# One more split pair from the start, seven more seven-product pairs, and the residual rows back in two halves

## The chip, the cores and the metric

The kernel runs on one core of a Trainium2 chip. A core has five engines that each work through their own list of instructions in order: PE (matmul), DVE (vector), ACT (scalar and activation), POOL (general) and SP, which here only starts DMAs. They meet through semaphores: an instruction waits until another engine has counted far enough, and everything behind it on its engine waits too. The metric is device time in microseconds of one execution, the median of several.

## The reference

One decoder layer on x of 256 tokens by 2048, in float32:

```python
u = RMSNorm(h);  lru_x, lru_gate, q, k, v, ret_gate = split(u @ w_in)
y = concat(RG-LRU(conv(lru_x)) * gelu(lru_gate),  retention(q, k, v) * silu(ret_gate))
h = h + y @ w_out                                  # 2048 x 2048
u = RMSNorm(h)
h = h + (silu(u @ w_gate) * (u @ w_up)) @ w_down   # 2048 x 5632 twice, 5632 x 2048
out = RMSNorm(h)
```

## The kernel before

**Precision.** Every float32 operand x is split into xh, a cast to a 32-bit matmul type (`fp32r`), and xl = x - xh. A product is three matmuls: ah bh, ah bl, al bh (`three`, L683 to L685). A weight tile thus comes as a DMA of 128 x 1024 into a raw tile (SP), is cast by ACT into `wh` (L123), and subtracted by DVE into `wl` (L124). Raw tiles rotate through 6 buffers, the pairs `wh`/`wl` through 4; from gate/up 1 to gate/up 9 there are 2 more of each (`raw2`, `split2`). A cast can start only when PE has read the last product from the pair that had the buffer before.

**Blocks.** The three late projections work on 2 x 2 blocks of the result (c11, c12, c21, c22, each 128 tokens by 512 columns, a bank of PSUM): out has two blocks (0, 1), gate/up eleven (0 to 10; c11 and c21 are gate, c12 and c22 up), down two (0, 1). A "quad" is one step along the contraction: 256 rows of weights by 1024 columns, two raw loads b11, b12 and b22, b21, against a left of a11, a12, a21, a22. A plain quad is eight products, 24 matmuls. A pair that is "summed" needs seven (Strassen in Winograd's form), 21 matmuls, and for that four sums of lefts (`sh`, `sl`) and four DVE adds of raw weights (`add`, L661), a split more, and a reload of half the weights.

**Sharing.** The products that several summed pairs of a block have in common are accumulated ahead, while the block before is still in work. `STEPS` gives for each block a string of steps: p is a plain quad, h half of one, s the "shared" part of a summed pair of the *next* block (four products, four raw adds, splits of 512, 512, 1024 and 512 columns), d the "direct" part of a pair of this block (three products, one load, one split of 1024). After the last s the results are combined (`share`, L806 to L811): p1 is a copy of c11 by ACT (L806), p = c12 - p1 and q = p - c22 by DVE (L807, L808), then q is copied by ACT back onto c12's PSUM tile (L809), and DVE forms c22 and c21 (L810, L811). PE's plain and direct products are then added onto these tiles; its first product onto c12 must wait for the copy L809. I call the step from one block to the next a handover. `SUMMED` lists the summed pairs: 2 in out 1, 2 in gate/up 0, 3 in gate/up 1, 4 in each of gate/up 2 to 9, 3 in gate/up 10, 3 shared ones (0, 1, 2) ahead of down 0. In down 5 more pairs are summed in block 0 and 7 in block 1, each as a `Quad` with all its seven products in one step (`SUMMED_DOWN`, in the order `ORDER_DOWN`).

**After a block.** In out, `post` adds the result to the residual rows (htok, DVE, L597), squares them (ACT), stores them to memory (`kept_rows`) and transposes them for gate/up (`turn`: PE into `ht`, ACT to `hf`, then cast and split, `ah` and `al`). In gate/up ACT forms silu (`gated`, L874), DVE multiplies (L876), PE transposes, ACT copies (`ff`, L867). Before down all eight row tiles (256 KB each) and the weights of the last norm are loaded back by POOL's queue (`swap_back`); `down_post` adds and normalises.

**Order.** The program is a list of steps. Loads are emitted three ahead of the step in work (`AHEAD`), and a scheduler that goes through the steps with its own timeline fixes the order of instructions on each engine when the kernel is built. On the chip each engine keeps to that order.

## Time and profile before

| | before |
|---|---|
| median of 3 runs | 1082.41 us (1081.9 to 1084.11) |
| profiled execution | 1082.46 us, span 1080.7 us |
| PE busy | 1070.2 us, 99%, 5089 matmuls |
| DVE busy | 964.1 us, 89% |
| ACT busy | 664.5 us, 61% |
| PE waits in all | 2.8 us |
| DMA | 244.62 MB, mean 226 GB/s |

Busy is the share of the span in which an engine had an instruction in work. A matmul counts as busy until its modelled end, though the next starts earlier, so 99% says that PE hardly stood still, not that it ran at its peak. In a timeline a row has the start in us, the duration, engine, line, operation and tiles (out<-in), and in brackets the idle time before it with what ended it. A row of waits has the waiting line, the one waited for, and the us in total, the times and the longest. The clock granted to PE was full throughout.

### The profile page before, as it was taken

To read this page: it belongs to the slowest core of one execution; us is meant where nothing else is said; L and a number is where in the kernel's file an instruction comes from. 1 tells how busy PE (TensorE), PEld (TensorE's weight loads), DVE (VectorE), ACT (ScalarE), POOL (GpSimd) and SP (SyncE) were. 2 spreads that over 40 slices of the span, in tenths; PEclk is the share of its full clock that TensorE was granted. 3 is DMA by queue.
4 is the path that set the end of the run, shared out by engine and by line. 5 is a ranking of instruction groups with operands and counts; after the bars stand their busy time and mean duration, and the time that the engine had idled before them with its cause. 6 is when DMAs were issued, how large, how long until landed. Compare 5 with 4: busy or idle time off the path is not lost.

```text
span 1080.7 us, 14590 instructions
## 1 busy us (share of the span) xinstructions
PE 1070.2 (99%) x5089; PEld 897.7 (83%) x5089; DVE 964.1 (89%) x1399; ACT 664.5 (61%) x947; POOL 57.2 (5%) x73
## 2 busy tenths in 40 slices
PE   9999999999999999999999999999999999999997
PEld 7888888888888888888888888888888888888886
DVE  7889789988878889989999999999999889997886
ACT  7666644468756676656656565665656656654563
POOL 0602230000000000000000000000002000000001
PEclk9999999999999999999999999999999999999999
DMA  9965475554556588677776777777767856474662
GB/s 325 336 213 171 159 254 166 183 176 158 192 195 234 183 304 273 231 235 256 257 270 228 251 260 242 263 269 232 258 234 270 289 181 214 162 245 159 214 212 101
DMA packets 71386, 244.62 MB, mean 226 GB/s; under 512 B 8208, under 2 KB 8592, under 8 KB 71312
## 3 DMA queue, kind: packets, MB, share of 16 engines
q1 hardware_dynamic: 68400, 236.34, 64.6%
q0 software_dynamic: 1472, 4.72, 1.3%
q10 hardware_dynamic: 1440, 2.62, 0.6%
q8 instruction: 40, 0.66, 0.2%
q14 instruction: 34, 0.28, 0.1%
HBM read 239.46 MB, written 4.19 MB: 225 GB/s over the span
## 4 chain that ended last, share of the span: by engine, by line
PE 98%; DVE 1%; DMA 1%; POOL 0%; SPq 0%; ACT 0%; issue 0%; POOLq 0%; ACTq 0%
PE c L685 22%; PE c L683 22%; PE c L684 22%; PE fm L194 11%; PE fm L196 5%; PE tm L174 3%; PE tm L175 3%; PE tm L176 3%; PE p L683 1%; PE p L685 1%; PE p L684 1%; PE ft L865 1%; DMA x<-in_x 1%; PE ht L588 0%; PE sc L492 0%; DVE wl L124 0%
## 5 line engine op out<-in xcount | busy, mean ns | idle before, releaser
L123 ACT CAST wh<-raw 128x1024 fp32r<-128x1024 f32 (+1 forms) x498 | 462.9, 959 | 323.8 <-PE c L685 130.8
L124 DVE TENSOR_TENSOR wl<-raw,wh 128x1024 fp32r<-128x1024 f32 (+1 forms) x498 | 542.2, 1115 | 72.5 <-ACT wh L123 71.2
L684 PE MATMUL c<-wl,ah 128*128 128x512 f32 x826 | 322.7, 391 | 0.0
L685 PE MATMUL c<-wh,al 128*128 128x512 f32 x826 | 321.8, 390 | 0.0
L683 PE MATMUL c<-wh,ah 128*128 128x512 f32 x826 | 280.3, 391 | 0.0
L683 PEld LDWEIGHTS c<-wh,ah 128*128 128x128 f32 x826 | 155.1, 188 | 32.0 <-ACT wh L123 0.3
L685 PEld LDWEIGHTS c<-wh,al 128*128 128x128 f32 x826 | 155.2, 188 | 31.8
L684 PEld LDWEIGHTS c<-wl,ah 128*128 128x128 f32 x826 | 155.2, 188 | 31.6
L194 PE MATMUL fm<-u,wh 128*128 128x512 f32 x512 | 161.4, 396 | 0.0
L196 PEld LDWEIGHTS fm<-u,wl 128*128 128x128 f32 x512 | 96.1, 188 | 22.4
L196 PE MATMUL fm<-u,wl 128*128 128x256 f32 x512 | 101.2, 279 | 0.0
L661 DVE TENSOR_TENSOR raw<-raw,raw 128x512 f32<-128x512 f32 x114 | 78.4, 689 | 2.0
L661 DVE TENSOR_TENSOR raw<-raw 128x512 f32<-128x512 f32 x114 | 78.3, 688 | 1.4
L194 PEld LDWEIGHTS fm<-u,wh 128*128 128x128 f32 x512 | 78.4, 189 | 0.3
L684 PE MATMUL c<-wl,sh 128*128 128x512 f32 x192 | 74.3, 390 | 0.0
L685 PE MATMUL c<-wh,sl 128*128 128x512 f32 x192 | 73.7, 390 | 0.0
L683 PE MATMUL c<-wh,sh 128*128 128x512 f32 x192 | 67.3, 391 | 0.3 <-ACT sh L123 0.3
L176 PE MATMUL tm<-wh,u 128*128 128x512 f32 x128 | 48.7, 391 | 0.0
L175 PE MATMUL tm<-wl,u 128*128 128x512 f32 x128 | 48.7, 393 | 0.0
L174 PE MATMUL tm<-wh,u 128*128 128x512 f32 x128 | 46.9, 394 | 1.4 <-ACT u L298 1.4
L683 PEld LDWEIGHTS c<-wh,sh 128*128 128x128 f32 x192 | 36.1, 188 | 8.1 <-ACT sh L123 0.7
L685 PEld LDWEIGHTS c<-wh,sl 128*128 128x128 f32 x192 | 36.1, 188 | 7.5
(247 smaller groups left out, 1027.4 us busy)
## 6 DMA issues: line engine op xcount, KB each, us to landing
raw<-in_w_gu SPq DMA_DIRECT2D x216, 512.0 KB, 5.3
raw<-in_w_down SPq DMA_DIRECT2D x91, 512.0 KB, 4.6
raw<-in_w_out SPq DMA_DIRECT2D x34, 512.0 KB, 3.7
raw<-in_w_lx SPq DMA_DIRECT2D x16, 512.0 KB, 6.4
raw<-in_w_k SPq DMA_DIRECT2D x16, 512.0 KB, 3.6
raw<-in_w_q SPq DMA_DIRECT2D x16, 512.0 KB, 4.2
raw<-in_w_rg SPq DMA_DIRECT2D x16, 512.0 KB, 3.5
raw<-in_w_lg SPq DMA_DIRECT2D x16, 512.0 KB, 3.5
```

Source lines behind the costliest of these rows:

```text
L123: act.copy(out=dst_h, in_=src)
L124: v.tensor_tensor(out=dst_l, in0=src, in1=dst_h.bitcast(F32), op=ALU.subtract)
L174: pe.matmul(ps, ah, wh, start=first, stop=False)
L175: pe.matmul(ps, ah, wl, start=False, stop=False)
L176: pe.matmul(ps, al, wh, start=False, stop=last)
L194: pe.matmul(ps, wh, hl, start=n + i == 0, stop=False)
L196: pe.matmul(ps[:, :S], wl, hl[:, :S], start=False, stop=n + i == len(order) - 1)
L661: v.tensor_tensor(out=dst, in0=a, in1=b, op=ALU.add)
L683: pe.matmul(p, ah, bh, start=first, stop=False, skip_group_check=onto)
L684: pe.matmul(p, ah, bl, start=False, stop=False, skip_group_check=onto)
L685: pe.matmul(p, al, bh, start=False, stop=last, skip_group_check=onto)
L865: pe.transpose(pt[:, o : o + P], g[:, (2 * b + c) * P : (2 * b + c) * P + P], ident)
```

## The change

- `SUMMED`, `STEPS`: out 1 gets four summed pairs (4 to 7) for two, gate/up 0 three (1, 2, 3) for two, gate/up 1 and gate/up 10 four for three: five more pairs with seven products. The steps of the blocks that host the shared parts change with them.
- Down 1 gets two more summed pairs, 12 and 19, and an order in which summed and plain quads alternate. The sums of these two lefts, made in down 0 for pairs 12 and 19, are kept in a pool of their own (`sums`) until step 7 of down 1.
- Pools: one more split pair, `split_near`, from out 0 to step 5 of down 1; one more split pair and two raw tiles, `split_far` and `raw_far`, from gate/up 1 to step 6 of down 0. Before it was two and two from gate/up 1 until the start of gate/up 10. The rows' pool moves to the other side of the memory, and a pad of 96 bytes stands ahead of it.
- The rows come back in two halves of four tiles: after step 9 of down 0 and after step 7 of down 1; the weights of the last norm after step 8 of down 1.

In the program as built PE has 21 matmuls fewer, all of 512 columns. DVE has 28 more raw adds, 19 more splits of 512 and 2 of 1024 columns, and 8 sums of 128 columns; ACT 19 more casts of 512 and 2 of 1024; SP 5 more loads of 512 KB. Split and raw tiles start at multiples of 128 bytes in both programs. All lines move by 5 to 8: L123 becomes L128, L661 L666, L806 L813, L809 L816.

```diff
--- before.py
+++ after.py
@@ -29,16 +29,17 @@
 
-SUMMED = ((), (4, 5), (2, 3), (1, 2, 3)) + ((0, 1, 2, 3),) * 8 + ((1, 2, 3),)
-SUMMED_OUT, SUMMED_FFN = (4, 5), (0, 1, 2, 3)
+SUMMED = ((), (4, 5, 6, 7), (1, 2, 3)) + ((0, 1, 2, 3),) * 10
+SUMMED_OUT, SUMMED_FFN = (4, 5, 6, 7), (0, 1, 2, 3)
 
 PLAIN = ((4, 5, 6, 7, 0, 1, 2, 3),) * 2 + (tuple(range(8)),) * 11
-STEPS = ("pppspppspp", "ppspdpsdpp", "pdpsdpspspp", "pspsdpsdpsdp") + ("psdhsdhsdhsdhp",) * 7 + ("psdpsdpsddp", "psdpsdpsdpp")
+STEPS = ("ppspspspsppp", "psdpsdpsddp", "pspsdpsdpsdp") + ("psdhsdhsdhsdhp",) * 9 + ("psdpsdpsddp",)
 
 EARLY_DOWN = (0, 1, 2)
-SUMMED_DOWN = (9, 12, 15, 17, 19), (5, 7, 9, 11, 13, 15, 17)
-ORDER_DOWN = (3, 4, 0, 5, 6, 1, 7, 8, 2) + tuple(range(9, 22)), tuple(range(22))
+SUMMED_DOWN = (9, 12, 15, 17, 19), (5, 7, 9, 11, 12, 13, 15, 17, 19)
+ORDER_DOWN = (3, 4, 0, 5, 6, 1, 7, 8, 2) + tuple(range(9, 22)), (0, 12, 1, 19, 2, 5, 3, 7, 4, 9, 6, 11, 8, 13, 10, 15, 14, 17, 16, 18, 20, 21)
+BESIDE = (12, 19)
 
 @with_exitstack
@@ -48,14 +49,17 @@
 
     cpool = ctx.enter_context(tc.tile_pool(name="consts", bufs=1))
     apool = ctx.enter_context(tc.tile_pool(name="acts", bufs=60))
+    edge = ctx.enter_context(tc.tile_pool(name="edge", bufs=1, side="right"))
+    edge.tile([P, 24], F32, name="edge_pad")
+    kept_stack = ctx.enter_context(ExitStack())
+    xpool = kept_stack.enter_context(tc.tile_pool(name="resid", bufs=8, side="right"))
     rpool = ctx.enter_context(tc.tile_pool(name="raw", bufs=6))
     wpool = ctx.enter_context(tc.tile_pool(name="split", bufs=4))
     early = ctx.enter_context(ExitStack())
-    xpool = early.enter_context(tc.tile_pool(name="resid", bufs=8))
     epool = early.enter_context(tc.tile_pool(name="conv", bufs=2))
     tpool = early.enter_context(tc.tile_pool(name="tmp", bufs=6))
-    late, resid, more, turn_of = [], [xpool], [], [0, 0]
-    extra = ExitStack()
+    late, resid = [], [xpool]
+    more_raw, more_split, counts = [], [], [0, 0]
     pmm = ctx.enter_context(tc.tile_pool(name="pmm", bufs=4, space=PSUM))
     paux = ctx.enter_context(tc.tile_pool(name="paux", bufs=4, space=PSUM))
 
@@ -72,14 +76,15 @@
         return resid[0].tile([P, 512], dt, tag="xh", name=nm(name))
 
     def split_tiles():
-        turn_of[1] += 1
-        pool_ = more[1] if more and turn_of[1] % 3 == 0 else wpool
-        return [pool_.tile([P, 1024], F32R, tag=g, name=nm(g)) for g in ("wh", "wl")]
+        counts[0] += 1
+        n = counts[0] % (4 + len(more_split))
+        p = more_split[n - 4] if n >= 4 else wpool
+        return [p.tile([P, 1024], F32R, tag=g, name=nm(g)) for g in ("wh", "wl")]
 
     def raw_tile():
-        turn_of[0] += 1
-        pool_ = more[0] if more and turn_of[0] % 4 == 0 else rpool
-        return pool_.tile([P, 1024], F32, tag="raw", name=nm("raw"))
+        counts[1] += 1
+        p = more_raw[0] if more_raw and counts[1] % 4 == 0 else rpool
+        return p.tile([P, 1024], F32, tag="raw", name=nm("raw"))
 
     def late_tile(name, dt=F32):
         return late[0].tile([P, 512], dt, tag="late", name=nm(name))
@@ -551,7 +556,7 @@
 
         names = ("a11", "a21", "a12", "a22", "s1", "s2", "s3", "s4")
 
-        def __init__(self, f, sums):
+        def __init__(self, f, sums, place=act_tile):
             self.h, self.l = [act_tile("ah", F32R)], [act_tile("al", F32R)]
             split(self.h[0], self.l[0], f)
             if sums:
...
@@ -726,6 +731,8 @@
 
         for i in range(n):
             program.append(([quads[i]], step(i)))
+            if i in hooks[ordered]:
+                program.append(([], hooks[ordered][i]))
 
         def end():
             with tc.manual_schedule(engines={nc.tensor.engine}) if ordered else ExitStack():
@@ -902,7 +909,8 @@
 
     def make_left(p):
         if dl[p] is None:
-            dl[p] = Left(ff[p], p in EARLY_DOWN + SUMMED_DOWN[0] + SUMMED_DOWN[1])
+            place = sum_tile if p in BESIDE else act_tile
+            dl[p] = Left(ff[p], p in EARLY_DOWN + SUMMED_DOWN[0] + SUMMED_DOWN[1], place)
 
     def down_block(d, ahead):
         ps = {} if d else ahead.ps
...
@@ -1094,23 +1102,58 @@
     for n in range(NLRU):
         fm_tile(Unit(A["w_lg"][n]), u, range(KT), lambda ps, n=n: lru_out(n, ps))
 
-    def swap():
+    near, far = ExitStack(), ExitStack()
+
+    def near_begins():
 
         early.close()
-        more.append(extra.enter_context(tc.tile_pool(name="raw2", bufs=2)))
-        more.append(extra.enter_context(tc.tile_pool(name="split2", bufs=2)))
-
-    def stop_more():
-        more.clear()
-
-    def swap_back():
-        extra.close()
-        late.append(ctx.enter_context(tc.tile_pool(name="late", bufs=4)))
-        resid[0] = ctx.enter_context(tc.tile_pool(name="resid2", bufs=8))
-        for key in [(cb, t) for cb in range(4) for t in range(2)]:
+        more_split.append(near.enter_context(tc.tile_pool(name="split_near", bufs=1, reuse_waits="tile")))
+
+    def near_stops():
+        more_split.clear()
+
+    def near_ends():
+        near.close()
+        late.append(ctx.enter_context(tc.tile_pool(name="late", bufs=4, reuse_waits="tile")))
+        load_fw()
+
+    def far_begins():
+
+        kept_stack.close()
+        more_split.append(
+            far.enter_context(tc.tile_pool(name="split_far", bufs=1, side="right", reuse_waits="tile"))
+        )
+        more_raw.append(
+            far.enter_context(tc.tile_pool(name="raw_far", bufs=2, side="right", reuse_waits="tile"))
+        )
+
+    def far_stops():
+        more_split.pop()
+        more_raw.clear()
+
+    beside, sums_kept = ExitStack(), []
+
+    def sum_tile(name, dt):
+        return sums_kept[0].tile([P, 512], dt, tag="sum", name=nm(name))
+
+    def rows_back(d):
+        resid[0] = ctx.enter_context(tc.tile_pool(name=f"resid_{d}", bufs=4, side="right", reuse_waits="tile"))
+        for key in [(cb, t) for cb in (2 * d, 2 * d + 1) for t in range(2)]:
             htok[key] = res_tile("htok")
             pool.dma_start(out=htok[key], in_=kept[key])
-        load_fw()
+
+    def far_ends():
+        far.close()
+        rows_back(0)
+        sums_kept.append(
+            beside.enter_context(tc.tile_pool(name="sums", bufs=4, side="right", reuse_waits="tile"))
+        )
+
+    def sums_end():
+        beside.close()
+        rows_back(1)
+
+    hooks = {0: {6: far_stops, 9: far_ends}, 1: {5: near_stops, 8: near_ends, 7: sums_end}}
 
     blocks = [Block(d, lambda i, d=d: A["w_out"][8 * d + i], y, out_post(d), STEPS[d], SUMMED[d]) for d in range(2)]
     blocks += [
@@ -1119,12 +1162,11 @@
     ]
     down = Block(NB + 2, lambda i: A["w_down"][i], dl, None, "", EARLY_DOWN, make_left)
     for b, after in zip(blocks, blocks[1:] + [down]):
+        if b.index == 0:
+            program.append(([], near_begins))
         if b.index == 3:
-            program.append(([], swap))
-        if b.index == NB + 1:
-            program.append(([], stop_more))
+            program.append(([], far_begins))
         b.put(after)
-    program.append(([], swap_back))
 
     for d in range(2):
         down_block(d, down)
```

Three places at handovers, as the built orders have them. First ACT at the handover from gate/up 9 to 10, from before, where c12_1588 is the tile that q is copied onto and wh_1630 and wh_1633 are the first weights that PE multiplies onto it:

```order
L123 CAST wh_1630_7774<-raw_1629_7772 128x1024
L123 CAST wh_1633_7789<-raw_1632_7787 128x1024
L123 CAST wh_1641_7808<-raw_1635_7793 128x512
L123 CAST ah_1636_7795<-ff_925_4524 128x512
L809 COPY c12_1588_7574<-q_1625_7750 128x512
L123 CAST wh_1646_7850<-raw_1635_7793 128x1024
L123 CAST wh_1651_7860<-raw_1650_7858 128x1024
```

The same place in the changed program, ACT, where the tile is c12_1614 and the first weights are wh_1664:

```order
L128 CAST wh_1664_7882<-raw_1663_7880 128x1024
L128 CAST ah_1670_7906<-ff_954_4622 128x512
L128 CAST wh_1685_7971<-raw_1684_7969 128x1024
L128 CAST wh_1692_8015<-raw_1691_8013 128x1024
L816 COPY c12_1614_7651<-q_1659_7858 128x512
```

and PE there:

```order
L690 MATMUL c22_1531_7270<-wh_1655_7840,al_872_4227 128x512
L688 MATMUL c22_1531_7270<-wh_1661_7867,ah_871_4226 128x512
L689 MATMUL c22_1531_7270<-wl_1662_7868,ah_871_4226 128x512
L690 MATMUL c22_1531_7270<-wh_1661_7867,al_872_4227 128x512
L688 MATMUL c11_1611_7639<-wh_1664_7882,ah_859_4190 128x512
L688 MATMUL c12_1614_7651<-wh_1664_7882,ah_859_4190 128x512
```

Before, two later casts (wh_1646, wh_1651) stood behind the copy; now two that take the buffers of wh_1655 and wh_1661 stand ahead of it, and PE reads these for the last time 5 and 2 matmuls ahead of its first product onto c12_1614.

Second, at the handover from gate/up 10 to down, ACT in the changed program; c12_1700 is down's c12, wh_1754 its first weight tile and ah_1752 its first left:

```order
L128 CAST wh_1767_8328<-raw_1766_8326 128x1024
L128 CAST wh_1757_8282<-raw_1756_8280 128x1024
L128 CAST wh_1754_8267<-raw_1751_8261 128x1024
L128 CAST wh_1770_8334<-raw_1769_8332 128x1024
L128 CAST ah_1752_8263<-ff_1037_5002 128x512
L128 CAST wh_1782_8391<-raw_1776_8376 128x1024
L816 COPY c12_1700_8037<-q_1747_8239 128x512
```

and PE there:

```order
L690 MATMUL c21_1699_8033<-wh_1732_8175,sl_1728_8151 128x512
L690 MATMUL c12_1700_8037<-wh_1729_8154,sl_1728_8151 128x512
L690 MATMUL c22_1612_7643<-wh_1743_8221,al_872_4227 128x512
L688 MATMUL c22_1612_7643<-wh_1749_8248,ah_871_4226 128x512
L689 MATMUL c22_1612_7643<-wl_1750_8249,ah_871_4226 128x512
L690 MATMUL c22_1612_7643<-wh_1749_8248,al_872_4227 128x512
L688 MATMUL c11_1697_8025<-wh_1754_8267,ah_1752_8263 128x512
```

Six casts stand here ahead of the copy, and wh_1757, which takes the buffer of wh_1732, stands ahead of wh_1754, the first tile that PE wants.

Third, DVE at the handover from out 1 to gate/up 0, before; c22_775 and c21_776 are gate/up 0's tiles, the htok rows those that out 1 adds to:

```order
L807 TENSOR_TENSOR p_802_3940<-c12_777_3814,p1_801_3939 128x512
L124 TENSOR_TENSOR wl_806_3951<-raw_804_3948,wh_805_3950 128x1024
L124 TENSOR_TENSOR wl_809_3966<-raw_807_3963,wh_808_3965 128x1024
L808 TENSOR_TENSOR q_803_3941<-p_802_3940,c22_775_3806 128x512
L124 TENSOR_TENSOR wl_812_3972<-raw_810_3969,wh_811_3971 128x1024
L810 TENSOR_TENSOR c22_775_3806<-q_803_3941,c21_776_3810 128x512
L811 TENSOR_TENSOR c21_776_3810<-c21_776_3810,p_802_3940 128x512
L124 TENSOR_TENSOR wl_815_4002<-raw_813_3999,wh_814_4001 128x1024
L597 TENSOR_TENSOR htok_611_3053<-c11_677_3369,htok_611_3053 128x512
L597 TENSOR_TENSOR htok_623_3114<-c21_679_3377,htok_623_3114 128x512
```

and in the changed program, where they are c22_791 and c21_792 and the first weights wl_836 and wl_839:

```order
L129 TENSOR_TENSOR wl_839_4089<-raw_837_4086,wh_838_4088 128x1024
L602 TENSOR_TENSOR htok_617_3075<-c11_677_3360,htok_617_3075 128x512
L602 TENSOR_TENSOR htok_629_3136<-c21_679_3368,htok_629_3136 128x512
L129 TENSOR_TENSOR wl_842_4095<-raw_840_4092,wh_841_4094 128x512
L602 TENSOR_TENSOR htok_640_3194<-c12_680_3372,htok_640_3194 128x512
L602 TENSOR_TENSOR htok_652_3255<-c22_678_3364,htok_652_3255 128x512
L666 TENSOR_TENSOR raw_840_4092<-raw_840_4092 128x512
L814 TENSOR_TENSOR p_829_4048<-c12_793_3873,p1_828_4047 128x512
L129 TENSOR_TENSOR wl_836_4074<-raw_834_4071,wh_835_4073 128x1024
L666 TENSOR_TENSOR raw_840_4092<-raw_840_4092,raw_849_4148 128x512
L815 TENSOR_TENSOR q_830_4049<-p_829_4048,c22_791_3865 128x512
L666 TENSOR_TENSOR raw_849_4148<-raw_840_4092,raw_849_4148 128x512
```

The combinations of gate/up 0 stood ahead of the adds onto htok; now p and q, the split wl_836 and three raw adds stand behind them.

More of the change, by code (lines that the diff above doesn't have):

```diff
@@ L564, in __init__ @@
                 v.tensor_tensor(out=s4, in0=a12, in1=s2, op=ALU.subtract)
-                self.h.append(act_tile("sh", F32R))
-                self.l.append(act_tile("sl", F32R))
+                self.h.append(place("sh", F32R))
+                self.l.append(place("sl", F32R))
                 split(self.h[1], self.l[1], g)
@@ L975, in down_post @@
         src = h if src is None else src
-        f = fw[cb][:, c0 : c0 + cw]
+        f = None if cb < 2 else fw[cb][:, c0 : c0 + cw]
         n = cb + (c0 > 0)
@@ L982, in down_post @@
             if cb < 2:
-                defer(13 + 2 * cb + t, lambda: v.tensor_tensor(out=h, in0=h, in1=f, op=ALU.mult))
+                defer(13 + 2 * cb + t, lambda: v.tensor_tensor(out=h, in0=h, in1=fw[cb], op=ALU.mult))
                 return
```

## The prediction

> **What bounds the kernel now.** I read the page first, then the waits of PE (the matmul engine), then timelines at one handover between blocks.
>
> ```profile
> span 1080.7 us, 14590 instructions
> PE 1070.2 (99%) x5089; PEld 897.7 (83%) x5089; DVE 964.1 (89%) x1399; ACT 664.5 (61%) x947; POOL 57.2 (5%) x73
> PEclk9999999999999999999999999999999999999999
> PE 98%; DVE 1%; DMA 1%; POOL 0%; SPq 0%; ACT 0%; issue 0%; POOLq 0%; ACTq 0%
> ...
> PE tm L174 <- ACT u L298: 1.4, 2, 1.0
> PE warm L116 <- DVE eps_t L109: 1.1, 1, 1.1
> PE c L683 <- ACT sh L123: 0.3, 1, 0.3
> ```
>
> PE is busy 99% of the span, the chain that ended last is 98% PE, and PE's whole list of waits is 2.8 us, 2.5 of them at the start. So the time is the number of matmuls times their spacing, and every wait that the change brings onto PE is paid in full. DVE, at 89%, is close behind.
>
> ```profile
> 600.79 0.39 PE L684 MATMUL c<-wl,ah 128*128 128x512 f32 x1
> 601.02 0.39 PE L685 MATMUL c<-wh,al 128*128 128x512 f32 x1
> ...
> 601.92 0.39 PE L685 MATMUL c<-wh,al 128*128 128x512 f32 x1
> ...
> 603.74 0.62 PE L683 MATMUL c<-wh,ah 128*128 128x512 f32 x2
> ...
> 370.74 0.40 PE L683 MATMUL c<-wh,sh 128*128 128x512 f32 x1
> 371.43 0.50 PE L683 MATMUL c<-wh,sh 128*128 128x512 f32 x1 [0.30 <-ACT sh L123]
> ```
>
> Five spacings from 600.79 to 601.92 are 1.13 us, so one matmul of 512 columns costs 0.227 us, while its result is complete 0.39 us after its start. The last two rows are the one stall in the middle of the run: 0.69 us from start to start, 0.46 too many.
>
> Next, what a step costs ACT (ScalarE) and DVE (VectorE), from the same handover:
>
> ```profile
> 587.39 4.42 ACT L123 CAST wh<-raw 128x1024 fp32r<-128x1024 f32 x5 [3.19 <-PE c L685]
> 591.72 0.61 ACT L123 CAST t4h<-raw 128x512 fp32r<-128x512 f32 x1
> 592.24 1.05 ACT L123 CAST wh<-raw 128x1024 fp32r<-128x1024 f32 x1
> 593.19 0.57 ACT L806 COPY p<-c 128x512 f32<-128x512 f32 x1
> ...
> 600.76 1.05 ACT L123 CAST wh<-raw 128x1024 fp32r<-128x1024 f32 x1 [3.86 <-PE c L685]
> 601.72 0.58 ACT L809 COPY c<-q 128x512 f32<-128x512 f32 x1
> ...
> 588.48 1.22 DVE L124 TENSOR_TENSOR wl<-raw,wh 128x1024 fp32r<-128x1024 f32 x1 [0.35 <-ACT wh L123]
> ...
> 594.83 2.35 DVE L124 TENSOR_TENSOR wl<-raw,wh 128x1024 fp32r<-128x1024 f32 x2
> 597.10 0.69 DVE L807 TENSOR_TENSOR p<-c,p 128x512 f32<-128x512 f32 x1
> ...
> 599.44 0.68 DVE L808 TENSOR_TENSOR q<-p,c 128x512 f32<-128x512 f32 x1
> 600.04 0.69 DVE L661 TENSOR_TENSOR raw<-raw 128x512 f32<-128x512 f32 x1
> 600.64 0.69 DVE L810 TENSOR_TENSOR c<-q,c 128x512 f32<-128x512 f32 x1
> ```
>
> Start to start in a queue, ACT takes 0.52 us for a cast of 512 and 0.95 for one of 1024 (1.05 until it is done); the copy L809 is done after 0.58. DVE takes 0.60 for 512 columns (0.69 until done) and, half of 597.10 - 594.83, 1.135 for a split of 1024 (1.23 until done). A cast begun at 587.39 for 1.05 is over at 588.44 and the DVE split behind it starts at 588.48: some 0.05 us per hand-over. The ACT rows also show what is fragile. The copy of q onto the tile c12 stands in ACT's queue behind a cast that waited 3.86 us for PE to give up a split buffer. It ended at 602.30, and PE's first product onto that tile starts at 603.96 (second matmul of the 603.74 row): 1.66 us to spare, 7 matmuls.
>
> **The change part by part.** The counts below compare the two built orders.
>
> *PE: 21 matmuls fewer, all of 512 columns.* 21 x 0.227 = 4.76 us gained, if PE never waits. The Trainium skill, "TensorE: Matmul & The Clock Gate", Part 1, gives a back-to-back gap of 512 columns / 2.4 GHz + 2.5 ns, 215.7 ns; by it the gain would be 4.5 us. The row above says 227 ns, and I use that.
>
> *DVE and ACT: more to do.*
>
> ```profile
> L661 DVE TENSOR_TENSOR raw<-raw,raw 128x512 f32<-128x512 f32 x114 | 78.4, 689 | 2.0
> L124 DVE TENSOR_TENSOR wl<-raw,wh 128x512 fp32r<-128x512 f32 x106 | 71.4, 686 | 6.4 <-ACT wh L123 6.3
> L564 DVE TENSOR_TENSOR s<-ff,s 128x128 f32<-128x128 f32 x12 | 3.5, 288 | 0.1
> 466.00:507.00 41.00, 41.00 (x187) 33.96 (x186) 39.47 (x51) 26.12 (x36) 0.00 (x0) 1.00 0.71 235
> 1000.00:1040.00 40.00, 40.00 (x179) 33.13 (x178) 34.62 (x40) 21.70 (x24) 0.00 (x0) 1.00 0.64 211
> ```
>
> DVE gets 28 more raw adds, 19 more splits of 512 and 2 of 1024, and 8 small sums of 128 columns: 47 x 0.60 + 2 x 1.135 + 8 x 0.29 = 33 us. ACT gets 19 x 0.52 + 2 x 0.95 = 11.8 us. In the windows (columns: window, PE, PEld, DVE, ACT, POOL, clock, DMA share, GB/s) DVE already fills 39.47 of 41.00 us in a gate/up block of four pairs, and PE does not wait there. Averages leave room for the 33 us. The places that don't are the handovers, where an engine may not start until PE frees a buffer, and PE then reads the result a few matmuls later. There I add up the queue between the two, with the rows above, for the orders shown with the change.
>
> *Gate/up 9 to 10.* The copy onto c12_1614 now stands behind wh_1685 and wh_1692. wh_1685 takes the buffer of wh_1655 (six pairs in turn), which PE reads last five matmuls before the product that needs the copy: 5 x 0.227 = 1.13 us. ACT needs 0.39 + 0.95 + 0.95 + 0.58 = 2.87. PE waits 1.74.
>
> *Gate/up 8 to 9.* The same: wh_1599, t4h_1596, wh_1606, then the copy; 0.39 + 0.95 + 0.52 + 0.95 + 0.58 = 3.39 against 11 matmuls, 2.49. Wait 0.90.
>
> *Gate/up 10 to down.* wh_1757 waits for the buffer of wh_1732, free six matmuls (1.36) before PE wants ah_1752; behind wh_1757 ACT does wh_1754, wh_1770 and ah_1752: 0.39 + 3 x 0.95 + 0.61 = 3.85. Wait 2.49. Then wh_1782 and the copy of c12_1700 end at 0.39 + 3 x 0.95 + 0.52 + 0.95 + 0.58 = 5.29, wanted after 9 matmuls and the first wait, 2.04 + 2.49 = 4.53: 0.76 more. DVE does p and q (p needs the matmul behind the freeing one), wl_1758, two combinations, wl_1755, wl_1771 and al_1753 by 0.62 + 2 x 0.60 + 1.135 + 2 x 0.60 + 2 x 1.135 + 0.69 = 7.11, against 14 matmuls and both waits, 6.42: 0.69 more. Together 3.94.
>
> *Out 1 to gate/up 0*, where two pairs became four in out and two became three in gate/up.
>
> ```profile
> L258 ACT ACT_TABLE_LOAD x4 | 5.1, 1283 | 0.1
> L591 ACT ACTIVATE hf<-ht,small 128x256 f32<-128x256 f32 x16 | 6.7, 467 | 0.4 <-PE ht L588 0.4
> 817.84 0.60 PE L865 MATMUL ft<-ident,gated 128*128 128x128 f32 x4
> ```
>
> In DVE's new order the four adds onto htok stand ahead of p, wl_836 and the two combinations; they stood behind them. From the finishing matmul of c11_677: 0.39 + wl_839 1.135 + seven operations of 512, 4.2, + wl_836 1.23 = 6.96. PE has 17 matmuls of 512 and 16 transposes (the 817.84 row: 0.60 for four, 0.11 apart), 3.85 + 1.76 = 5.61. Wait 1.35. Then raw add, q, raw add and c22 end 2.40 later, PE wants c22 after 5 matmuls, 1.13: 1.27 more. Further on ACT has two casts, the copy, a cast, the table load of 1.28, t4h, two hf, a cast and ah_859 in one queue, some 7.3 us after c22's first raw add; PE's use of ah_859 lies 6.6 after it: 0.7. Before all this, in out 1, a chain of ACT (four casts and two hf) and DVE (nine operations) lies between PE's release of wh_806 and the cast wh_823: 0.39 + 2.4 + 4.8 + 1.05 = 8.7 against 34 matmuls, 7.7: 1.0. Together 4.3, the least certain term.
>
> *Gate/up 2 to 3.* wh_1097 waits for wh_1077's buffer; then wl_1098, add, wl_1109, add, p, half a split and wl_1101 on DVE: 0.39 + 1.05 + 2 x 1.135 + 4 x 0.60 + 1.23 = 7.34 against 30 matmuls, 6.80: 0.54. Then q and wl_1114, 1.74 against three matmuls, 0.68: 1.06. Together 1.6.
>
> *The end of down 0.* An add onto htok and two raw adds now stand in DVE's queue just ahead of a split, wl_1954, that PE wants next; no margin in the rows says how much of it shows, between nothing and one operation of 0.60: I take half, 0.3.
>
> Sum of waits: 1.74 + 0.90 + 3.94 + 4.3 + 1.6 + 0.3 = 12.8. They cross between engines some 25 times at 0.05: 1.2 more, 14.0. The old stall of 0.46 goes, since the order around it is new.
>
> *At nothing.* The start of the split and raw tiles: the built addresses were multiples of 128 before too. Five more loads and the rows back in halves:
>
> ```profile
> raw<-in_w_gu SPq DMA_DIRECT2D x216, 512.0 KB, 5.3
> raw<-in_w_down SPq DMA_DIRECT2D x91, 512.0 KB, 4.6
> htok<-kept_rows POOLq DMA_DIRECT2D x8, 256.0 KB, 8.1
> ACT bh L123 <- DMA raw<-in_w_down: 22.4, 8, 4.2
> ```
>
> The DMA engines are used at 0.64 and 0.71 in the two windows, five loads of 5.3 us are spread over five blocks, and rows that take 8.1 us to land come back a dozen steps of about 5 us before they are added to. If that cover fails it is in down 1: with seven-product quads ACT there waits on the loads (the last row, up to 4.2 us), and two more such quads plus four rows and the norm weights fall on the same stretch. Bounds: 0 to 3 us; I take 0, because ACT waits there without PE waiting now. The other bound for the waits: nothing at all if the lead of five or six pairs absorbs them, and less than nothing is excluded, since PE has no other waits to lose; above, half as much again, 21 us (1098).
>
> Forecast: the profiled execution took 1082.46 (span 1080.7 and 1.8 around it), 0.05 above the median of 1082.41. 1082.46 - 4.76 - 0.46 + 14.0 = 1091.2. **1091.2 us, slower by 0.8%.**
>
> **The rivals.**
>
> A. *The matmul count decides.* For it: no steady block of before lets PE wait with DVE at 96%. Against: the rows show only 1.66 us to spare at a handover with one cast ahead of the copy, and now there are two or three. 1082.46 - 4.76 = 1077.7, faster.
>
> B. *The waits come at half*, since casts reach their buffers earlier than I count or two of the terms feed on the same lateness: 1082.46 - 5.2 + 7 = 1084.3, no difference that shows (0.2%, 2.2 us, is what a measurement of this kernel tells from no change).
>
> C. *Down 1 starves as well*: raw loads late once per added seven-product quad, up to 3 us: 1094.
>
> D. *The clock drops after the new waits.* The Trainium skill, in the same Part 1, has the clock halved after an idle window of about 3.4 us. As a mechanism here: seven handovers at which the next 3.4 us of matmuls, 15 of them, take 0.227 longer each, 3.4 us: up to 24, and if one or two waits trigger it, 3.4 to 7, 1098. The row that bears on it:
>
> ```profile
> 6.00:10.00 4.00, 2.60 (x11) 1.51 (x10) 2.34 (x8) 2.97 (x7) 0.00 (x0) 1.00 0.84 293
> ```
>
> PE idled 1.4 of 4.0 us there at clock 1.00, and none of my waits passes 2.7.
>
> **How the numbers follow.** Forecast 0.67 (its own range 1087 to 1094.5), A 0.08, B 0.10, C 0.12, D 0.03. The 80% range runs from just under B to past C: 1083.5 to 1096. Faster 0.08 from A; same 0.08 from most of B; slower 0.84 from the rest.
>
> **What would show it.** Waits on PE of 10 to 15 us in all where there were 2.8, ending on ACT's casts or its copy L816 and on DVE's splits and combinations, at six places: the ends of out 1, of gate/up 2, 8, 9 and 10, and of down 0; the largest at the step into down, over 2 us. The blocks between as long as before or a little shorter. PE's instructions 21 fewer. The clock at 9 throughout. I am wrong if PE's waits stay under 5 us, or lie elsewhere: inside blocks, or in down 1 on DMA.

## The result: 15 us slower, further than forecast

| | before | changed |
|---|---|---|
| median | 1082.16 us (1081.9 to 1084.11, 4 runs) | 1097.86 us (1097.35 to 1098.67, 4 runs) |
| ratio | 1 | 1.014, 95% interval 1.0127 to 1.0152 |
| profiled execution, span | 1082.46 us, 1080.7 us | 1097.88 us, 1096.0 us |

The change is slower by 1.4%. The direction was forecast, the size was not: 1091.2 us was predicted, and 1097.86 lies 1.9 us above the upper end of the range.

The page of the changed kernel, and PE's list of waits:

```profile
span 1096.0 us, 14639 instructions
PE 1074.8 (98%) x5068; PEld 894.2 (82%) x5068; DVE 993.7 (91%) x1456; ACT 675.8 (62%) x968; POOL 56.3 (5%) x73
PE 88%; DVE 4%; DMA 3%; issue 2%; ACT 2%; POOL 0%; SPq 0%; POOLq 0%; ACTq 0%; DVEq 0%
...
PE c L688 <- ACT c L816: 3.0, 3, 2.0
PE c L688 <- ACT ah L128: 2.8, 2, 2.4
PE c L689 <- DVE wl L129: 2.5, 3, 1.2
PE c L688 <- ACT wh L128: 1.6, 3, 1.1
PE warm L121 <- DVE eps_t L114: 1.1, 1, 1.1
PE tm L179 <- ACT u L303: 1.0, 2, 0.6
PE p L688 <- ACT wh L128: 0.8, 2, 0.5
PE p L689 <- DVE wl L129: 0.2, 1, 0.2
```

PE lost 21 instructions, as counted. Its share of the chain that ended last fell from 98% to 88%, and DVE, DMA and ACT came into it. The listed waits are 13.0 us where there were 2.8.

A list of waits shows only time in which PE stood idle; matmuls overlap by 0.16 us (0.39 long, 0.227 apart), and a slow matmul is not idle. So I also summed, from the records of each trace, how much farther apart the starts of neighbouring matmuls are than the normal spacing of their size, by place. This "excess" is used from here on:

| place (us in the changed kernel) | predicted | excess, changed | excess, before |
|---|---|---|---|
| start to out 1 (0 to 360) | as before | 9.1 | 9.1 |
| out 1 to gate/up 0 and 1 (360 to 440) | 4.3 | 6.4 | 0.7 |
| gate/up 2 to 3 (520 to 560) | 1.6 | 1.9 | 0 |
| gate/up 8 to 9 (760 to 800) | 0.9 | 1.1 | 0 |
| gate/up 9 to 10 (800 to 840) | 1.7 | 2.3 | 0 |
| gate/up 10 to down (840 to 880) | 3.9 | 5.3 | 0 |
| end of down 0 (920 to 960) | 0.3 | 0 | 0 |
| down 1 (1000 to 1080) | 0 | 3.3 | 0 |

The predicted column is without the 1.2 us that were added for some 25 hand-overs. Measured, 19.6 us more (29.4 against 9.8), less 4.8 for the matmuls, plus 0.3 behind the last matmul, is 15.1 of the 15.3 us by which the span grew. So the places were right, but for the end of down 0 and down 1.

At the step into down, the costliest single wait, PE's and then ACT's timeline of the changed kernel read:

```profile
858.27 0.39 PE L690 MATMUL c<-wh,al 128*128 128x512 f32 x1
861.08 1.02 PE L688 MATMUL c<-wh,ah 128*128 128x512 f32 x3 [2.42 <-ACT ah L128]
862.51 0.50 PE L688 MATMUL c<-wh,ah 128*128 128x512 f32 x1 [0.41 <-ACT c L816]
862.85 1.60 PE L689 MATMUL c<-wl,ah 128*128 128x512 f32 x4
864.46 2.08 PE L690 MATMUL c<-wh,al 128*128 128x512 f32 x4
...
857.56 2.94 ACT L128 CAST wh<-raw 128x1024 fp32r<-128x1024 f32 x3 [1.29 <-PE c L690]
860.41 0.61 ACT L128 CAST ah<-ff 128x512 fp32r<-128x512 f32 x1
860.93 1.04 ACT L128 CAST wh<-raw 128x1024 fp32r<-128x1024 f32 x1
861.88 0.58 ACT L816 COPY c<-q 128x512 f32<-128x512 f32 x1
```

ACT stands until PE frees a buffer (857.56), does the three casts wh_1757, wh_1754 and wh_1770, then ah_1752, done at 861.02, and PE starts at 861.08. 2.81 us from 858.27 less 0.23 is an excess of 2.58, where the sum of the prediction had 2.49. The copy costs 0.63 more (predicted 0.76). What was not in the sum stands in the last two PE rows: four matmuls in 1.61 us and four in 1.87 (to 866.33) are 0.40 and 0.47 apart on average. The windows behind the waits at the step from out 1 to gate/up 0 and at this place show why; the third holds the end of the wait at gate/up 9 to 10 (the number behind POOL's 0.00 is the clock):

```profile
392.16:395.57 3.41, 3.30 (x8) 2.10 (x8) 3.41 (x8) 3.39 (x7) 0.00 (x0) 0.50 1.04 400
863.20:866.61 3.41, 3.40 (x9) 2.19 (x8) 3.41 (x5) 1.01 (x3) 0.00 (x0) 0.50 0.81 270
818.82:822.23 3.41, 2.65 (x12) 2.24 (x13) 3.41 (x6) 0.70 (x2) 0.00 (x0) 1.00 0.84 272
```

The clock granted to PE was halved for 3.41 us after two of the waits; after the wait of 2.1 us that ended at 819.58 it was not (the last section says what decides). Eight matmuls started 0.43 us apart in this execution.

In down 1 the chain that ended last begins, in the window 1010 to 1060, with the norm weights and goes on through weight loads and splits (start, duration, what):

```profile
1005.90 6.33 DMA fw<-in_final_norm_w
1012.22 0.02 issue
1012.25 0.83 DVE htok L992 x2
...
1024.14 4.96 DMA raw<-in_w_down
1029.10 0.02 issue
1029.12 0.63 ACT bh L128
1029.75 0.02 issue
1029.77 0.69 DVE bl L129
...
1034.69 5.63 DMA raw<-in_w_down
```

### The profile page after: what moved, and what is told of

Read it like the earlier page. It is cut to its first block, busy times and chain, and to the rows that moved or that the text cites. A ratio compares the mean times of both kernels' runs of the same rounds, so it can differ in the third digit from the quotient of the medians.

```text
span 1096.0 us, 14639 instructions
## 1 busy us (share of the span) xinstructions
PE 1074.8 (98%) x5068; PEld 894.2 (82%) x5068; DVE 993.7 (91%) x1456; ACT 675.8 (62%) x968; POOL 56.3 (5%) x73
## 4 chain that ended last, share of the span: by engine, by line
PE 88%; DVE 4%; DMA 3%; issue 2%; ACT 2%; POOL 0%; SPq 0%; POOLq 0%; ACTq 0%; DVEq 0%
PE c L689 20%; PE c L688 20%; PE c L690 20%; PE fm L199 11%; PE fm L201 5%; PE tm L179 3%; PE tm L181 3%; PE tm L180 3%; DMA raw<-in_w_down 2%; DVE wl L129 2%; ACT wh L128 1%; PE ft L872 1%; DVE raw L666 1%; DMA fw<-in_final_norm_w 1%; PE p L689 1%
## 5 line engine op out<-in xcount | busy, mean ns | idle before, releaser
L128 ACT CAST wh<-raw 128x1024 fp32r<-128x1024 f32 (+1 forms) x510 | 468.0, 952 | 300.0 <-PE c L690 103.0
L129 DVE TENSOR_TENSOR wl<-raw,wh 128x1024 fp32r<-128x1024 f32 (+1 forms) x510 | 550.2, 1106 | 56.7 <-ACT wh L128 55.7
L689 PE MATMUL c<-wl,ah 128*128 128x512 f32 x784 | 306.5, 392 | 2.5 <-DVE wl L129 2.5
L690 PE MATMUL c<-wh,al 128*128 128x512 f32 x784 | 304.1, 392 | 0.0
L688 PE MATMUL c<-wh,ah 128*128 128x512 f32 x784 | 272.3, 393 | 7.5 <-ACT c L816 3.0
L666 DVE TENSOR_TENSOR raw<-raw,raw 128x512 f32<-128x512 f32 x128 | 87.9, 687 | 1.9
L666 DVE TENSOR_TENSOR raw<-raw 128x512 f32<-128x512 f32 x128 | 87.3, 686 | 1.3
L689 PE MATMUL c<-wl,sh 128*128 128x512 f32 x214 | 82.7, 389 | 0.0
L690 PE MATMUL c<-wh,sl 128*128 128x512 f32 x214 | 81.8, 389 | 0.0
L688 PE MATMUL c<-wh,sh 128*128 128x512 f32 x214 | 75.1, 392 | 0.0
L689 PEld LDWEIGHTS c<-wl,sh 128*128 128x128 f32 x214 | 40.2, 188 | 8.3
```

Of the source, the lines that this page charges most:

```text
L128: act.copy(out=dst_h, in_=src)
L129: v.tensor_tensor(out=dst_l, in0=src, in1=dst_h.bitcast(F32), op=ALU.subtract)
L666: v.tensor_tensor(out=dst, in0=a, in1=b, op=ALU.add)
L688: pe.matmul(p, ah, bh, start=first, stop=False, skip_group_check=onto)
L689: pe.matmul(p, ah, bl, start=False, stop=False, skip_group_check=onto)
L690: pe.matmul(p, al, bh, start=False, stop=last, skip_group_check=onto)
```

## The experiments

Two theories. ORDER, the prediction's own: what PE waits for is the queue that the built order puts ahead of the needed cast, copy or split. LOAD: DVE, given 33 us more, is simply late. The ratios are to the kernel before on the same chip, whose median there is given.

**1. Only the pools and the rows.** The summed pairs and both orders go back:

```diff
-SUMMED = ((), (4, 5, 6, 7), (1, 2, 3)) + ((0, 1, 2, 3),) * 10
+SUMMED = ((), (4, 5), (2, 3), (1, 2, 3)) + ((0, 1, 2, 3),) * 8 + ((1, 2, 3),)
-SUMMED_DOWN = (9, 12, 15, 17, 19), (5, 7, 9, 11, 12, 13, 15, 17, 19)
+SUMMED_DOWN = (9, 12, 15, 17, 19), (5, 7, 9, 11, 13, 15, 17)
 (STEPS, SUMMED_OUT, ORDER_DOWN: as before)
```

> The changed kernel with the summed pairs, the steps and both orders of down as they were before: only the pools (near and far split pairs, far raw tiles), the rows in halves and the late norm weights are new. Same matmuls, adds, splits and casts as before. Two theories. LOAD: PE waits because DVE got 33 us more to do; then nothing is left here but down 1's late norm weights, 1082 to 1085 us. ORDER: any change of the buffers gives another order at the handovers between blocks, and the queue ahead of what PE wants next is a matter of that order; then PE waits at handovers here too, at other places than in the changed kernel, 1086 to 1100 us.

Measured: 1098.79 us against 1083.17, ratio 1.0144 (1.0114 to 1.0173). As slow as the whole change, with the instruction counts of the kernel before:

```profile
PE 1078.1 (98%) x5089; PEld 898.0 (82%) x5089; DVE 964.1 (88%) x1399; ACT 665.7 (61%) x947; POOL 56.4 (5%) x73
```

DVE's 964.1 us in 1399 instructions are those of before. So LOAD cannot be the whole cause. The excess lies at other places: 2.2 at 640 to 680, 0.5 at 680 to 720, 4.2 at 720 to 760, 2.5 at 840 to 880, and 7.5 in down 1. At the largest of the handovers:

```profile
730.38 0.39 PE L688 MATMUL c<-wh,ah 128*128 128x512 f32 x1
733.18 0.79 PE L689 MATMUL c<-wl,ah 128*128 128x512 f32 x1 [2.41 <-DVE wl L129]
...
729.58 1.82 DVE L129 TENSOR_TENSOR wl<-raw,wh 128x1024 fp32r<-128x1024 f32 x2
731.31 0.68 DVE L814 TENSOR_TENSOR p<-c,p 128x512 f32<-128x512 f32 x1
731.91 2.35 DVE L129 TENSOR_TENSOR wl<-raw,wh 128x1024 fp32r<-128x1024 f32 x2
```

PE wants a wl; DVE works on without a gap, and in its queue two other splits and p stand first.

**2. Only the pairs in down 1**, with the new pools and rows (`SUMMED` and `STEPS` as before, the rest as changed).

> The changed kernel with the summed pairs and steps of out and gate/up as before; the pools, the rows in halves and the two more pairs in down 1 stay. Six matmuls fewer than before (1.4 us). LOAD: DVE has only 8 adds and 2 splits more, all in down 1: 1081 to 1085 us, waits only in down 1, some 3 us as in the changed kernel. ORDER: handover waits as in the run with the pools alone, since everything up to down is the same program there: 1085 to 1098 us.

Measured: 1095.82, ratio 1.0116 (1.0087 to 1.0146). The excess in gate/up is that of run 1 (2.2, 0.4, 3.9, 2.5), with 0.7 more at 438, and down has 5.0.

**3. Only the pairs of out and gate/up**, in the kernel before with its own pools (`SUMMED`, `STEPS` and `SUMMED_OUT` as changed).

> The kernel before with the summed pairs and steps of out and gate/up of the change, and nothing else: its own pools, rows and down. 15 matmuls fewer (3.4 us). LOAD: five pairs' DVE work is there, so the waits from out 1 to gate/up 0 (5.7 us in the changed kernel) and most of the later handover waits (10.6) stay, and down 1 runs clean: 1082.2 - 3.4 + 13 to 16 = 1092 to 1095 us. If the POOLS are the cause: 1079 to 1082 us. ORDER: waits from out 1 to gate/up 0 as those blocks hold two pairs more, and waits at some later handovers but not the same ones: 1085 to 1097 us.

Measured: 1102.42, ratio 1.0177 (1.0148 to 1.0207), slower than the whole change and above what any theory had expected. Excess: 12.3 at 360 to 440, 1.0 at 440 to 480, 4.3 at 520 to 560, 5.1 at 840 to 880, 0.8 at 960 to 1000; 31 matmuls at the half clock, some 6 us of it. So 1 and 3 cost 15.6 and 19.3 us alone, and together, with the pairs of down 1, 15.7. The parts do not add up, as one would expect if each edit draws a new order.

**4. Relief for DVE.**

```diff
-            for dst, a, b in ((b11, b11, b12), (b12, b12, b22), (b22, b11, b22), (b21, b22, b21)):
-                v.tensor_tensor(out=dst, in0=a, in1=b, op=ALU.add)
+            for k, (dst, a, b) in enumerate(((b11, b11, b12), (b12, b12, b22), (b22, b11, b22), (b21, b22, b21))):
+                (pool if k in (3,) else v).tensor_tensor(out=dst, in0=a, in1=b, op=ALU.add)
```

> The changed kernel with one of the four raw adds of each summed pair (the last, b21 = b22 + b21) on POOL in place of DVE: 64 adds, 38 us of DVE work at 0.60, more than the 33 us that the change added; POOL takes 1.3 to 1.7 us for one by its rows of the same size. LOAD: nearly all waits at handovers and in gate/up go, 1077.7 plus down 1's 3.3 and a rest: 1079 to 1084 us. ORDER: a new order with waits elsewhere: 1085 to 1100 us. A rival for POOL: it is slower next to DVE than alone, and the split behind it is late: over 1100 us.

Measured: 1101.61, ratio 1.017 (1.014 to 1.0199). It cannot decide between the theories, since DVE got no relief:

```profile
L666 POOL TENSOR_TENSOR raw<-raw 128x512 f32<-128x512 f32 x64 | 132.0, 2063 | 740.5 <-DVE raw L666 562.7 <-DMA raw<-in_w_gu 54.5 <-ACT wh L128 41.7
...
L129 DVE TENSOR_TENSOR wl<-raw,wh 128x1024 fp32r<-128x1024 f32 x394 | 515.9, 1332 | 48.4 <-ACT wh L128 43.4 <-PE fm L201 4.3
```

An add takes POOL 2.06 us (DVE 0.69), and DVE's 394 splits of 1024 went from 1.23 us (477.2 us in the changed kernel) to 1.33, 38.7 us more: as much as the 64 adds had taken (64 x 0.60 is 38.4). In all DVE was busy for 1000.4 us, where the changed kernel has 993.7.

**5 and 6. The two halves of run 1.** First the rows: run 1 with all eight tiles and the norm weights at the start of down, the extra buffers stopped at the start of gate/up 10, and no pool for the sums (`BESIDE` is empty).

```diff
-    hooks = {0: {6: far_stops, 9: far_ends}, 1: {5: near_stops, 8: near_ends, 7: sums_end}}
+    hooks = {0: {}, 1: {}}
+        if b.index == NB + 1:
+            program.append(([], lambda: (more_split.clear(), more_raw.clear())))
         b.put(after)
+    program.append(([], lambda: (far.close(), rows_back(0), rows_back(1), near_ends())))
```

> The run with the pools alone, but all eight row tiles and the norm weights come back at the start of down and the extra buffers end there, as in the kernel before. If the late rows and norm weights are what makes down 1 wait, the 7.5 us of waits at 1000 to 1040 us go and those in gate/up (2.2 at 640, 0.5 at 680, 4.2 at 720) stay: some 7 us above the kernel before. If down 1 waits for want of buffers or by its order: over 12 us above it.

Measured: 1089.41 against 1083.41, ratio 1.0053 (1.0034 to 1.0071). Down 1 has no excess left, nor has 840 to 880; 2.2, 0.4 and 3.8 in gate/up stay, and 0.8 are new at 920 to 960, in down 0.

Then run 1 with the rotation alone:

```diff
-        p = more_split[n - 4] if n >= 4 else wpool
+        p = (more_split[counts[0] // 3 % 2] if counts[0] % 3 == 0 else wpool) if len(more_split) == 2 else more_split[n - 4] if n >= 4 else wpool
```

> The run with the pools alone, but while both extra split pairs are there the extra pairs are taken at every third split in turn, as before, and not as fifth and sixth of six. A pair is still taken again after six splits, so neither work nor buffers differ. ORDER: gate/up's handover waits (9.3 us at 640 to 880) go with the order, down 1's 7.5 us stay: some 8 us above the kernel before. If the gate/up waits come from the number or place of the buffers: unchanged, 15 us above it.

Measured: 1088.91 against 1083.41, ratio 1.0048 (1.003 to 1.0066). Every excess in gate/up is gone (below 0.1 in each 40 us from 320 to 960), 5.9 in down 1 stay. Run 1 had these waits of PE between 300 and 900, and in run 6 the list of that stretch is empty:

```profile
PE c L689 <- DVE wl L129: 3.4, 2, 2.4
PE c L688 <- ACT wh L128: 1.6, 1, 1.6
PE c L688 <- ACT ah L128: 0.3, 1, 0.3
```

The edit changes neither the work nor the number of buffers nor, while both pairs are there, after how many splits a pair is taken again. It changes the order: compared place by place, 188 of ACT's 947 instructions in the trace, 362 of DVE's 1399 and 1415 of PE's 5089 are others. That is ORDER in its plainest form.

What down 1 still waits for in run 6; the first row is POOL's, which issues the loads of the norm weights, the others are DVE's:

```profile
986.82 2.12 POOL L900 DMA_DIRECT2D fw<-in_final_norm_w  x4 [37.02 <-PE c L690]
...
991.19 0.69 DVE L129 TENSOR_TENSOR bl<-raw,bh 128x512 fp32r<-128x512 f32 x1 [4.32 <-ACT bh L128]
991.91 0.69 DVE L666 TENSOR_TENSOR raw<-raw 128x512 f32<-128x512 f32 x1
993.82 0.69 DVE L666 TENSOR_TENSOR raw<-raw,raw 128x512 f32<-128x512 f32 x1 [1.21 <-DMA raw<-in_w_down]
994.43 1.22 DVE L129 TENSOR_TENSOR wl<-raw,wh 128x1024 fp32r<-128x1024 f32 x1
995.57 1.28 DVE L992 TENSOR_TENSOR htok<-htok,fw 128x512 f32<-128x512 f32 x2
996.77 1.22 DVE L129 TENSOR_TENSOR wl<-raw,wh 128x1024 fp32r<-128x1024 f32 x1
997.91 1.28 DVE L992 TENSOR_TENSOR htok<-htok,fw 128x512 f32<-128x512 f32 x2
```

Four loads of norm weights start at 986.82 and a weight load at 986.90, which lands 6.83 us later by the chain. It is the third of a group on its queue; the third of the other groups in this down 1 takes 5.3 to 6.3, a load that meets nothing else 3.0. Beside the norm weights it is thus 0.5 to 1.5 us longer. DVE stands 4.32 us (for the second load of the group) and 1.21 us (for this one) and then has four multiplies of rows among the splits that PE wants; PE waits 2.5 us at 1001.7.

**7 and 8. Both edits, and one pair more.** Run 7 has both diffs. Run 8 adds pair 19 to the summed ones of down 1 (order 0, 1, 19, 2, 3, 5, 4, 7, ...), its two sums in a pool of two tiles in place of the near pair until step 3, when the norm weights are loaded.

> Both edits on the run with the pools alone: rows and norm weights at the start of down, extra pairs at every third split. If these two are the whole cause of its 15.6 us, PE waits for nothing after the start and even the stall of 0.46 at 371 us before may go: within 0.15% of the kernel before, on the fast side. If a third cause is left: more than 2 us above it.

> The kernel with both edits and one summed pair more in down 1 (19, its two sums kept in a pool of two tiles until step 3, where the norm weights then go). 3 matmuls fewer, 0.7 us. If a pair in down pays where the order is clean: 0.5 to 1.2 us below the kernel before (0.05 to 0.1%). If its sums and adds or the norm weights at step 3 make PE wait: 1 us or more above it.

Measured in 7: 1083.47 against 1083.41, ratio 0.9998 (0.9989 to 1.0007). The 15.6 us are gone, and nothing that can be measured is won. The new pools lie where they lay in run 1, so their place in memory is not the cause. In 8: 1082.71, ratio 0.9992 (0.9983 to 1.0001): the 0.7 us of three matmuls seems to arrive, but the interval touches 1. It is the best of the kernels run, and it is not shown to beat the one before.

**9. Only the norm weights.** Run 6 with

```diff
-    hooks = {0: {6: far_stops, 9: far_ends}, 1: {5: near_stops, 8: near_ends, 7: sums_end}}
+    hooks = {0: {6: far_stops, 9: far_ends, 12: near_stops, 15: near_ends}, 1: {7: sums_end}}
```

> The run with the extra pairs at every third split, and one edit more: the near pair stops at step 12 of down 0 and the norm weights come at step 15 there, before down 1; the rows stay in halves. If the norm weights are what hurts down 1 (their four loads start together with a weight load, which then takes 6.8 us in place of 3, and four multiplies pile up behind them on DVE), most of the 5.9 us of waits go: 0 to 2 us above the kernel before. If the rows in halves hurt: 5 us or more above it.

Measured: 1082.72 against 1082.93, ratio 0.9997 (0.9987 to 1.0006). No excess is left in down. With the pairs as before the rows in halves cost nothing; what cost in run 6 is the late end of the near pair together with the norm weights that wait for it. The run moves both and does not say how much each has of it.

**10. What the five pairs cost on a clean order.** Run 7 with `SUMMED`, `STEPS` and `SUMMED_OUT` of the change.

> The kernel with both edits (as fast as before) and the five new pairs of out and gate/up, 15 matmuls or 3.4 us fewer. LOAD, as the prediction had it for this one place: from out 1 to gate/up 0 DVE is at 98% of PE's time, so 5 to 7 us of waits stay there, and a new pair's block may wait once more: 2 to 6 us above the kernel before. ORDER: with clean pools the pairs cost nothing: 2 to 3.4 us below it.

Measured: 1085.51 against 1082.93, ratio 1.0022 (1.0012 to 1.0033). Excess: 5.4 at 360 to 400, 0.5 at 840 to 880, 0.9 at 920 to 960, elsewhere nothing. At that place the trace fits LOAD: DVE works without a pause (columns as in the other windows):

```profile
344.00:384.00 40.00, 38.86 (x178) 31.55 (x177) 37.77 (x62) 28.29 (x46) 0.00 (x0) 1.00 0.66 217
384.00:404.00 20.00, 17.59 (x83) 13.62 (x82) 19.82 (x35) 17.24 (x34) 0.00 (x0) 1.00 0.94 323
```

19.82 of 20.00 us are busy on DVE, PE has 17.59. PE's waits there end on DVE and on ACT. The pairs win 3.4 us of matmuls and lose 6.

**11. Three casts behind the copy.** The changed kernel, with `issue_after(copy)` around three loads, so that ACT's order at the step into down is

```order
L128 CAST wh_1754_8267<-raw_1751_8261 128x1024
L128 CAST ah_1752_8263<-ff_1037_5002 128x512
L818 COPY c12_1700_8037<-q_1747_8239 128x512
L128 CAST wh_1757_8282<-raw_1756_8280 128x1024
L128 CAST wh_1770_8334<-raw_1769_8332 128x1024
L128 CAST ah_1760_8288<-ff_1116_5368 128x512
L128 CAST wh_1782_8391<-raw_1776_8376 128x1024
```

> The changed kernel with three casts (wh_1757, wh_1770, wh_1782) put behind the copy of q onto c12_1700 on ACT at the step from gate/up 10 into down; ACT's order there is now wh_1754, ah_1752, the copy, wh_1757, wh_1770, and the work is the same. If the queue ahead of the copy and of ah_1752 makes PE wait there, as the prediction summed it, the 5.3 us at 840 to 880 fall to 2 to 3, and the half clock behind the 2.4 us wait goes too. If PE waits for DVE there, or the casts are wanted at once: 5 us or more stay.

Measured: at 840 to 880 the excess falls from 5.3 to 2.0, without the half clock:

```profile
858.56 1.05 ACT L128 CAST wh<-raw 128x1024 fp32r<-128x1024 f32 x1 [1.50 <-issue]
859.51 0.62 ACT L128 CAST ah<-ff 128x512 fp32r<-128x512 f32 x1
860.03 0.58 ACT L818 COPY c<-q 128x512 f32<-128x512 f32 x1
...
860.18 0.99 PE L690 MATMUL c<-wh,ah 128*128 128x512 f32 x2 [0.80 <-ACT ah L128]
```

Same work, same buffers, three casts moved: the mechanism at this place is shown. The kernel as a whole gained nothing: 1099.3, ratio 1.0142 (1.0127 to 1.0158). The wait that ends at 818.7, as long as in the changed kernel, was now followed by seven matmuls at the half clock (3.9 for 2.3 there):

```profile
818.89:822.30 3.41, 3.41 (x9) 2.74 (x10) 3.41 (x7) 0.00 (x0) 0.00 (x0) 0.50 0.85 262
```

The new order behind the three casts brought 3.0 us at 960 to 1000 and 4.1 in 1000 to 1080 for 3.3.

**12. The whole change with the old rotation** (the diff of run 6 on the changed kernel).

> The whole change with the extra pairs at every third split, as before. ORDER: the waits of gate/up that come from the rotation (1.9 at 520, 1.1 at 760, part of 2.3 at 800 and 5.3 at 840) fall by 4 to 6 us, those from out 1 to gate/up 0 (5.7) and in down (3.3) stay: 8 to 11 us above the kernel before. If the new pairs cause them: unchanged, 14 to 16 above it.

Measured: 1093.51 against 1082.93, ratio 1.0092 (1.0077 to 1.0107). The 5.3 us at 520, 760 and 800 are gone, 3.4 stay at 840, 7.6 at 360 to 440; down has 7.3 at 960 to 1080, more than before.

**13 and 14. Down 1 of the changed kernel.** Run 13 puts the four multiplies off (`defer(17 + 2 * cb + t, ...)` for 13), run 14 moves the norm weights up (near pair stopped at step 16 of down 0, weights after step 1 of down 1).

> The changed kernel with the four multiplies of rows by norm weights put off by four steps of the program, so that DVE does not stand for 1.1 us in front of them (the one wait of DVE for the norm weights in down 1). If that wait starts the lag of down 1, its 3.3 us fall to 1 or less. If the weight loads and DVE's order there make the lag, 2.5 to 4 us stay.

> The changed kernel with the norm weights loaded after step 1 of down 1 (the near pair stops at step 16 of down 0) and not after step 8. If their four loads beside the weight loads make the 3.3 us, these go, and the time is 2 to 3.5 us below the changed kernel. If the order of the summed quads in down 1 makes the waits, 3 us or more stay in down 0 and 1 together, at other places, since the missing pair gives another order again.

Measured in 13: 1097.36 against 1082.76, ratio 1.0139 (1.0117 to 1.0161). Down 1 has 2.0 for 3.3, but the edit did not do what it was for. In the traces ACT, DVE and PE do the same instructions, by line and tile, in the same order as in the changed kernel, and DVE still stood 1.0 us before the multiplies. So the run says nothing of the multiplies; it shows that one and the same order can have 3.3 us of excess in down 1 in one execution and 2.0 in another. In 14: 1101.47, ratio 1.018 (1.0165 to 1.0195): 7.6 us of excess in 960 to 1040. So late norm weights are not the one cause in the changed kernel: waits come without them too. Whether these come from its order of quads or from the near pair that now ends earlier, the run does not tell. How the 3.3 us divide is left open.

## Why the prediction was wrong

*Right:* PE's 21 matmuls and their 4.8 us; that every wait on PE would be paid in full; that DVE's average said nothing and the handovers decided; the six places but the end of down 0. The single waits came out as the queues had summed them: 2.58 for 2.49 and 0.63 for 0.76 at the step into down, 2.1 for 1.74 at gate/up 9 to 10, 0.77 for 0.90 at 8 to 9. Run 11 moved three casts behind the copy, and the wait fell from 2.4 to 0.8 us.

*Wrong:* the time is 6.7 us above the 1091.2; 3.3 of this are down 1, 3.0 the handovers, 0.3 the end behind the last matmul. The step that failed is "Bounds: 0 to 3 us; I take 0" for down 1. It cost 3.3 us (2.0 in run 13, with the same order), and rival C, which was that step, was given 0.12 as if it excluded the forecast, though it adds to it. The reason given, that ACT waits there without PE waiting now, did not ask how much was to spare. What failed there is not shown to be C's late loads: from 988 us on ACT waits as long for raw loads of down as before from 975 us on (22.8 us in seven waits, before 22.4 in eight), and the chain above runs through DVE's splits as well as through the loads. That the rows would return without cost was right with the pairs as before (run 9). The norm weights, which the argument names in the bound alone, come into it (runs 6 and 9), but do not explain it (run 14). What makes the 3.3 us stays open.

*Mis-sized:* the handovers' 14.0 us were 17.0 in excess (20.3 less the 3.3 of down 1). Rival D is part of it: eight matmuls came 0.2 us late each, 1.6 us, some of it hidden behind waits that would have come anyway. From out 1 to gate/up 1, run 11 has the same order with the clock at full, and 5.8 us of excess for 6.4. D too was weighed as a case of its own, at 0.03, since the wait at the start had left the clock at 1.00; and its price of 3.4 us a wait was twice too high, as 3.41 us at half clock hold eight matmuls at most. The Trainium skill, "TensorE: Matmul & The Clock Gate", Part 1, says of its window of about 3.4 us that it is free-running. The traces agree: each half clock lasts 3.41 us or twice that, and within an execution they start whole multiples of 3.413 us apart. They differ from the idle window of about 3.4 us that the prediction quoted: some 2 us of lost time in one such window were enough (last section), so my bound "none of my waits passes 2.7" was no protection. The rest of the 3.0 is mostly out 1 to gate/up 0, the term called least certain, 4.3 in the sum. One of its parts is also summed wrongly: 0.39 + 2.4 + 4.8 + 1.05 is 8.64 and not 8.7, a wait of 0.9 for 1.0.

*Right for another reason:* the forecast told a story in which the new pairs fill the queues. Run 1 shows that the pools and the late norm weights alone cost as much, with no instruction added. The waits summed were those of this one order. With a clean order the pairs leave those from out 1 to gate/up 0 (5.4 us, run 10); 5.3 us in gate/up go with the rotation (run 12). At the step into down 3.4 of the 5.3 us stay in run 12, with pairs and late pools together, and no run divides them further.

## What to carry to other kernels

Where one engine is at 99% and the order on the others is fixed at build, an edit that changes no work can cost a percent: read, at each step where a buffer or a tile changes hands, what the new order puts between the release and the use, and sum it with durations of the trace. Small costs that come on top of each other are added to the forecast and not listed as alternatives. And undo the parts of a change one at a time, the harmless-looking ones first.

## What the runs showed of the hardware

- The clock of PE halves for 3.41 us at a time; matmuls of 512 columns are then 0.427 us apart for 0.227. By the clock records of the 16 traces each such stretch ahead of the last matmul lasts 3.413 us, one 6.827, and within an execution they start whole multiples of 3.413 us apart: at 392.16 and 863.20 in the changed kernel (138 times), at 732.89 and 1012.78 in run 1 (82 times). So the time is cut into fixed windows, and their place differs from execution to execution. What decides is the excess inside one window. From 320 us on there are 21 stretches, and the window ahead of each holds at least 1.98 us of excess; of the windows at full clock that none follows, one holds 2.03 and the next 1.93. The wait of 2.1 to 2.2 us at gate/up 9 to 10 shows it: in run 11 it lies whole in the window 815.47 to 818.89, and the clock halves; in the changed kernel an edge at 818.82 cuts it, 1.37 and 0.75 us of it fall to the two sides, and the clock stays. In the same way a wait of 2.57 us halves it at 733 in run 1, while 2.60 at 733 in run 5 and 2.77 at 734 in run 2, cut by edges, do not.
- An add of 128 x 512 in float32 took POOL 2.06 us beside a busy DVE, and DVE's splits of 1024 columns became 8% slower over the run, 1.33 for 1.23 us.
- A weight load of 512 KB took 3.0 to 3.3 us when it met nothing, 5.3 to 6.3 as the third of a group on its own queue (runs 1 and 6, down 1), and as such a third 6.8 (run 6) and 8.5 (run 1) when four loads of norm weights on another queue started with it.
